# The second product of the attention scores over all 128 rows, in a two-layer decoder trunk

## The chip, the core and the metric

The kernel runs on one core of a Trainium2 chip, in one launch. The metric is the device time of that launch in microseconds (us), as the median of several runs; lower is better. The engines are TensorE (PE; its weight loads stand in a row of their own, PEld), VectorE (DVE), ScalarE (ACT), GpSimd (POOL) and SyncE (SP, which issues the loads from memory).

## What is computed

A trunk of two layers over 512 tokens of 1024 features, all float32: layer 0 is a gated linear recurrence and a gated FFN, layer 1 a differential attention and another gated FFN. The change lies in the scores of that attention. Each of its 8 heads has two components with keys and queries of 64 features each:

```python
def diff_attention(h, k, v, w_q, w_o, ..., rel_table, lambda_init):
    q = (h @ w_q).reshape(B, T, DA_HEADS, 2, DA_HEAD_DIM) * (DA_HEAD_DIM ** -0.5)   # 8 heads, 2, 64
    def block(args):                                                                # 128 tokens
        qb, bi = args
        bias = jnp.where((rel >= 0)[..., None], table[t5_bucket(rel)], -jnp.inf)
        s = jnp.einsum('bqhcd,bkhcd->bhcqk', qb, k) + bias
        p = jax.nn.softmax(s, axis=-1)
        attn = p[:, :, 0] - lam * p[:, :, 1]
        return jnp.einsum('bhqk,bkhv->bqhv', attn, v)
    ...
    o = rmsnorm(o, subln_g) * (1.0 - lambda_init)
    return o.reshape(B, T, DA_VDIM_TOTAL) @ w_o
```

## The kernel before

Everything is kept with the features on the 128 partitions and the 512 tokens along the row. To multiply float32 numbers exactly enough, a number is split into a high and a low part, both float32r, and a product is three matmuls: high by high, low by high, high by low (`mm3`, lines 102 to 104).

`attention` has a manual schedule: the instructions of PE, DVE, ACT and POOL run in the order in which the code issues them. First come the keys and queries of head 0. Then a loop goes over 32 blocks (8 heads of 4 blocks of 128 queries; block i of a head looks at its first n = 128 (i + 1) keys). In one turn, `scores(b + 2)` issues the scores of a block, `weigh(b + 1)` forms the attention weights on DVE (line 982), `turn(b)` transposes them on PE (line 989; ACT copies them back, line 991) and `gather(b)` multiplies them with the values (line 1002). Between these steps `units` issues pieces of the large products: keys K, queries Q and values V of the next heads, later the output product. Each of these needs a weight tile that SP loads, POOL multiplies by a gain (line 84), ACT rounds to the high part (line 756) and DVE subtracts for the low part (line 759). When a K or Q product is complete, DVE scales it out of PSUM (`evac`, line 825), and its parts are formed by steps that `some` issues one by one.

The queries of a head are a tile of two components, `qs`: component c has its high part on its own 64 rows and its low part on the other 64. The high part of the keys, `kh`, has for each component the same 64 features on both halves of the rows (ACT line 846, POOL line 847). So the first matmul of a component, line 958, contracts 128 rows and gives high by high and low by high at once. The low part of the keys, `kl`, is one tile of 128 rows by 512: rows 0 to 63 are component 0, rows 64 to 127 component 1 (DVE line 853). The second matmul, line 959, contracts 64 rows: the high part of the queries with the low part of the keys, added to the same PSUM bank. A block thus issues four matmuls in a row: 958, 959 for component 0, then 958, 959 for component 1. `kl` comes from a pool of two buffers.

Of the kernel before, what the change touches and what calls it, by code (L numbers as in the profile page):

```python
# [11 lines left out]
F32 = mybir.dt.float32  # L12
F32R = mybir.dt.float32r
# [21 lines left out]
class Trunk:  # L35
# [17 lines left out]
    def split(self, x, hi, lo, gain=None):  # L53
        """hi + lo = x (times gain), exact to float32, both in float32r."""
# [9 lines left out]
    def x_split(self, n, g, pool=None):  # L64
        """x^T tile n times a norm's gain, as two float32r parts"""
        pool = pool or self.xp
        g = None if g is None else self.gain(g, n)
        hi = pool.tile([P, T], F32R, tag="xs", name=f"xh{n}", bufs=2 * KD)
        lo = pool.tile([P, T], F32R, tag="xs", name=f"xl{n}", bufs=2 * KD)
        self.split(self.x[n], hi, lo, g)  # L70
        return hi, lo

    def stage(self, src, width=1024, gain=None, k0=0, cols=P):
        """weights from memory, times a gain of their input features"""
# [24 lines left out]
    def mm3(self, out, s, m, start, stop):  # L99
        """three passes of split operands; s stationary (hi, lo), m moving (hi, lo)."""  # L100
# [5 lines left out]
    def banks(self, ctx, name, **tags):  # L106
        """PSUM for a phase: tag -> (tiles, banks in a tile)"""
# [15 lines left out]
    def proj_first(self, items, xs, last, between=()):  # L123
        """several products at once, all but the last input tile first; between them, what else PE has to do"""
# [7 lines left out]
    def norm_steps(self, acc, name, tag):  # L132
        """the two parts of a norm as steps for proj_first; its result lands in the list"""
# [5 lines left out]
    def sq_add(self, acc, x, first, now=True):  # L139
        """acc += x^2; the sum is returned where it is not to be issued now"""  # L140
# [9 lines left out]
    def rsqrt_steps(self, out, ms, n):  # L150
        """out = ms ** -0.5 over the whole range: a guess from the exponent, three Newton steps"""
# [25 lines left out]
    def sums(self, acc, tag, chunks=range(4)):  # L177
        """sums over the features, by token"""
# [5 lines left out]
    def by_column(self, out, col):  # L184
        """out[p, t] = col[t] on every partition"""
# [40 lines left out]
    def begin(self, xs, acc, f_ps, q_ps):  # L226
        """the stream, its parts and its squares; head 0's first two products as the pieces come in"""
# [45 lines left out]
    def hgrn(self, xs, acc, on_tile):  # L273
        tc, nc, a, sp = self.tc, self.nc, self.a, self.sp
        v, s = nc.vector, nc.scalar
        with ExitStack() as ctx:
# [5 lines left out]
            # lower bound: softmax of two logits, first row; 1 - lb is the second  # L282
# [40 lines left out]
            def prep(h, f_ps, q_ps):  # L323
                """decay factors, keys and queries of every level."""
# [14 lines left out]
                # blocks of 4: types q0 q1 q2 q3 c1 c2 a2 c3 b3 a3, each over the 128 blocks  # L339
# [9 lines left out]
                # products over the blocks and what follows a place in its block  # L349
# [11 lines left out]
                # blocks of 16: types c0 c1 c2 c3 a2 a3 b3, each [32 blocks, 4 places]  # L361
# [5 lines left out]
                t4 = n16(tot)  # [p, child, block of 16]  # L367
# [19 lines left out]
                # blocks of 32, 64, 128  # L387
# [17 lines left out]
            def intra(h, vt, r1, r2, qs, ks, tt):  # L405
# [22 lines left out]
                # states at the chunks' ends  # L428
# [15 lines left out]
                # scores^T [key place, token], by chunk  # L444
# [4 lines left out]
                # level 1: ten types of 8 blocks  # L449
# [74 lines left out]
    def residual(self, w_src, ys, kt, on_tile, rb=None, late=False, extra=(), between=(), final=None):  # L524
        """x^T += (w^T y^T) (times rb by token); late: the last input tile comes last"""
# [30 lines left out]
    def last_tile(self, w_src, ys, kt, acc, out):  # L556
        """the last tile of the stream and the final norm, by halves of the tokens"""
# [32 lines left out]
        def factor(half):  # L590
            """1/rms of 256 tokens, as rsqrt but by column"""
# [17 lines left out]
        def spread(r):  # L609
            """for DVE and, in another bank, for the copy that GpSimd reads"""  # L610
# [89 lines left out]
    def bias_vector(self):  # L700
        """kept once for each of 128 tokens, so that a place less per token is a plain stride"""
# [544 lines left out]
```

## Time and profile before

| | |
|---|---|
| median of 3 runs | 1295.34 us (1295.14 to 1296.74) |
| span of the profiled execution | 1292.2 us |
| PE busy | 1263.4 us, 98% |
| PEld busy | 1043.4 us, 81% |
| DVE busy | 869.5 us, 67% |
| ACT busy | 568.1 us, 44% |
| POOL busy | 109.2 us, 8% |

The profile is of one execution. Its span runs from the first to the last instruction that the profiler saw; no other time is given for that execution, so what lies around the span is known only as the difference from the median, 1295.34 - 1292.2 = 3.1 us. A matmul's end is modelled, so PE's busy share says little on how tightly matmuls follow each other: for that the starts of successive rows are read. The attention's loop lies between about 664 and 898 us of the span.

### The profile page before, as it was taken

To read this page: it belongs to the slowest core of one execution; us is meant where nothing else is said; L and a number is where in the kernel's file an instruction comes from. 1 tells how busy PE (TensorE), PEld (TensorE's weight loads), DVE (VectorE), ACT (ScalarE), POOL (GpSimd) and SP (SyncE) were. 2 spreads that over 40 slices of the span, in tenths; PEclk is the share of its full clock that TensorE was granted. 3 is DMA by queue.
4 is the path that set the end of the run, shared out by engine and by line. 5 is a ranking of instruction groups with operands and counts; after the bars stand their busy time and mean duration, and the time that the engine had idled before them with its cause. 6 is when DMAs were issued, how large, how long until landed. Compare 5 with 4: busy or idle time off the path is not lost.

```text
span 1292.2 us, 18027 instructions
## 1 busy us (share of the span) xinstructions
PE 1263.4 (98%) x6994; PEld 1043.4 (81%) x6994; DVE 869.5 (67%) x1627; ACT 568.1 (44%) x986; POOL 109.2 (8%) x89
## 2 busy tenths in 40 slices
PE   8999899999999999999999999999999999999997
PEld 7888798778888888888887778787788888888886
DVE  7978689586777777523367878866687777772223
ACT  5554455454444444322245545554454444442221
POOL 3000000020000000000233332200200000000001
PEclk9999899999999999999999999999999999999999
DMA  6225322133333333333332212212233333333321
GB/s 207 82 84 82 100 69 80 50 114 99 98 98 98 96 96 95 93 90 90 94 98 61 78 50 57 74 59 65 76 120 99 98 98 98 98 90 90 91 88 66
DMA packets 37949, 115.35 MB, mean 89 GB/s; under 512 B 4032, under 2 KB 9448, under 8 KB 37864
## 3 DMA queue, kind: packets, MB, share of 16 engines
q1 hardware_dynamic: 36968, 113.29, 29.8%
q8 instruction: 55, 0.90, 0.3%
q10 hardware_dynamic: 896, 0.92, 0.2%
q14 instruction: 30, 0.25, 0.1%
HBM read 110.52 MB, written 3.67 MB: 88 GB/s over the span
## 4 chain that ended last, share of the span: by engine, by line
PE 57%; issue 30%; DVE 8%; DMA 3%; ACT 2%; SPq 0%; POOL 0%; POOLq 0%; DVEq 0%; ACTq 0%
PE mm L102 16%; PE mm L103 16%; PE mm L104 16%; DMA wst<-in_w_fqg_dram 2%; PE sc L959 1%; PE po L1002 1%; DVE wlo L58 1%; PE sc L958 1%; DVE wlo L759 1%; DVE sd L457 1%; DVE kl L853 1%; PE tp L989 1%; ACT whi L57 0%; DMA x<-in_x_t_dram 0%; PE sc L103 0%
## 5 line engine op out<-in xcount | busy, mean ns | idle before, releaser
L102 PE MATMUL mm<-xh,whi 128*128 128x512 f32 x1008 | 399.7, 397 | 0.5 <-ACT whi L57 0.5
L103 PE MATMUL mm<-xl,whi 128*128 128x512 f32 x1008 | 394.7, 392 | 2.5 <-DVE xl L61 2.3
L104 PE MATMUL mm<-xh,wlo 128*128 128x512 f32 x1008 | 394.3, 391 | 2.3 <-DVE wlo L58 2.3
L58 DVE TENSOR_TENSOR wlo<-wst,whi 128x1024 fp32r<-128x1024 f32 (+2 forms) x182 | 216.0, 1191 | 165.8 <-ACT whi L57 163.4
L57 ACT CAST whi<-wst 128x1024 fp32r<-128x1024 f32 (+2 forms) x182 | 181.8, 1003 | 257.5 <-PE mm L103 192.4
L104 PEld LDWEIGHTS mm<-xh,wlo 128*128 128x128 f32 x1008 | 189.8, 188 | 43.0 <-DVE wlo L58 3.4
L103 PEld LDWEIGHTS mm<-xl,whi 128*128 128x128 f32 x1008 | 190.1, 189 | 41.9 <-DVE xl L61 4.7
L102 PEld LDWEIGHTS mm<-xh,whi 128*128 128x128 f32 x1008 | 189.8, 188 | 41.0 <-issue 1.5
L102 PE MATMUL mm<-hh,whi 128*128 128x512 f32 (+1 forms) x374 | 142.8, 382 | 0.0
L103 PE MATMUL mm<-hl,whi 128*128 128x512 f32 (+1 forms) x374 | 142.6, 381 | 0.0
L104 PE MATMUL mm<-hh,wlo 128*128 128x512 f32 (+1 forms) x374 | 142.6, 381 | 0.0
L667 DVE TENSOR_TENSOR u<-mm,rbc_f 128x512 f32<-128x512 f32 x88 | 60.2, 688 | 73.5 <-PE mm L104 73.5
L147 POOL TENSOR_TENSOR acc<-acc,sq 128x512 f32<-128x512 f32 x18 | 26.7, 1482 | 669.2 <-ACT sq L146 669.1
L102 PEld LDWEIGHTS mm<-hh,whi 128*128 128x128 f32 x374 | 70.1, 188 | 15.2
L104 PEld LDWEIGHTS mm<-hh,wlo 128*128 128x128 f32 x374 | 70.1, 188 | 15.2
L103 PEld LDWEIGHTS mm<-hl,whi 128*128 128x128 f32 x374 | 70.1, 188 | 15.1
L669 ACT ACTIVATE c<-u,pack 128x512 f32<-128x512 f32 x88 | 71.5, 816 | 7.7 <-DVE u L667 4.0
L102 PE MATMUL mm<-whi,xh 128*128 128x256 f32 x256 | 74.7, 293 | 0.0
L103 PE MATMUL mm<-wlo,xh 128*128 128x256 f32 x256 | 72.4, 283 | 0.2 <-DVE wlo L759 0.2
L57 ACT CAST hh<-c 128x512 fp32r<-128x512 f32 x44 | 27.2, 619 | 102.9 <-DVE c L678 102.9
L104 PE MATMUL mm<-whi,xl 128*128 128x256 f32 x256 | 72.3, 283 | 0.0
L671 DVE SCALAR_TENSOR_TENSOR c<-u,pack,c 128x512 f32<-128x512 f32 x88 | 66.1, 751 | 2.8
(258 smaller groups left out, 1718.8 us busy)
## 6 DMA issues: line engine op xcount, KB each, us to landing
wst<-in_w_up_dram SPq DMA_DIRECT2D x88, 512.0 KB, 3.6
wst<-in_w_down_dram SPq DMA_DIRECT2D x32, 512.0 KB, 3.6
wst<-in_w_fqg_dram SPq DMA_DIRECT2D x22, 512.0 KB, 4.4
wst<-in_w_kq_dram SPq DMA_DIRECT2D x16, 512.0 KB, 3.7
wst<-in_w_down_dram SPq DMA_DIRECT2D x16, 384.0 KB, 3.2
wst<-in_w_i_dram SPq DMA_DIRECT2D x8, 512.0 KB, 4.4
wst<-in_w_ao_dram SPq DMA_DIRECT2D x8, 512.0 KB, 4.0
wst<-in_w_v_dram SPq DMA_DIRECT2D x8, 512.0 KB, 3.6
```

Source lines behind the costliest of these rows:

```text
L57: i = nc.scalar.copy(hi, x)
L58: j = nc.vector.tensor_tensor(lo, x, hi.bitcast(F32), ALU.subtract)
L102: mm(out, s[0], m[0], start=start, stop=False)
L103: mm(out, s[0], m[1], start=False, stop=False)
L104: mm(out, s[1], m[0], start=False, stop=stop)
L147: add = lambda engine=nc.vector: engine.tensor_tensor(acc, acc, sq, ALU.add)
L457: v.copy_predicated(dst, m, src)
L667: v.tensor_tensor(u[:, 2:], ps, rb, ALU.mult)
L669: s.activation(c, u[:, 2:], AF.Identity, bias=self.cb[:, layer, n:n + 1], scale=w(2))
L671: v.scalar_tensor_tensor(c, u[:, 0:T], w(0), c, ALU.mult, ALU.add)
L759: v.tensor_tensor(me.w[1], me.st, me.w[0].bitcast(F32), ALU.subtract)
L853: v.tensor_tensor(lo[own], k[own], hi[own, c].bitcast(F32), ALU.subtract))
```

## The change

The low part of the keys becomes a tile of two components, each 128 rows by 512: component c has the low part on its own 64 rows and zeros on the other 64. There are two such tiles, one for even and one for odd heads, allocated once; their zeros are written once by POOL before the loop, and DVE writes only the rows of each component's own half. The second matmul now contracts all 128 rows: the queries' high part meets the keys' low part, and the queries' low part meets zeros. The diff also strips comments and docstrings, which is left out here; with the added lines, 958 and 959 become 961 and 962, and 847 becomes 851.

```diff
             lower, upper = slice(0, 64), slice(64, 128)
             parts = ((lower, upper), (upper, lower))
+            kls = [ap.tile([P, 2, T], F32R, tag=f"kl{i}", name=f"kl{i}", bufs=1) for i in range(2)]
+            for t in kls:
+                for c, (own, other) in enumerate(parts):
+                    nc.gpsimd.memset(t[other, c].bitcast(F32), 0.0)
...
             def keys(h, ps):
                 k = evac(ps)
                 hi = ap.tile([P, 2, T], F32R, tag="kh", name="kh")
-                lo = ap.tile([P, T], F32R, tag="kl", name="kl")
+                lo = kls[h % 2]
...
                 for c, (own, other) in enumerate(parts):
                     side.append(lambda c=c, own=own:
-                                v.tensor_tensor(lo[own], k[own], hi[own, c].bitcast(F32), ALU.subtract))
+                                v.tensor_tensor(lo[own, c], k[own], hi[own, c].bitcast(F32), ALU.subtract))
...
                 for c in range(2):
-                    row = slice(64 * c, 64 * c + 64)
                     mm(sc[c], qs[h][:, c, oi], ks[h][0][:, c, 0:n], start=True, stop=False)
-                    mm(sc[c], qs[h][row, c, oi], ks[h][1][row, 0:n], start=False, stop=True)
+                    mm(sc[c], qs[h][:, c, oi], ks[h][1][:, c, 0:n], start=False, stop=True)
```

On PE, this is the order around the scores of a head's second block, rows of the kernel before with - and of the change with + (`sc` are the scores in PSUM, the shape is that of the result; how many rows are contracted does not show here):

```order
 L103 MATMUL mm<-wlo,xh_5497 128x256
 L104 MATMUL mm<-whi,xl_5498 128x256
-L958 MATMUL sc<-kh,qs 128x256
-L959 MATMUL sc<-kl,qs 128x256
-L958 MATMUL sc<-kh,qs 128x256
-L959 MATMUL sc<-kl,qs 128x256
+L961 MATMUL sc<-kh,qs 128x256
+L962 MATMUL sc<-kl_5943,qs 128x256
+L961 MATMUL sc<-kh,qs 128x256
+L962 MATMUL sc<-kl_5943,qs 128x256
```

Nothing moved on PE: the same matmuls stand at the same places, and the low part of the keys is now the fixed tile. On DVE, ACT and SP the order is the same too.

On POOL, this is the order at the start of the attention, ahead of and behind the clearing of the bias tile `nb` (`wst` is a weight tile times its gains, `kh` the copy of the keys' high part to the other half of the rows):

```order
 L84 TENSOR_TENSOR wst<-wst,gains 128x1024 x2
 L741 MEMSET nb 128x2x256
+L824 MEMSET kl_5943 64x512 x2
+L824 MEMSET kl_5944 64x512 x2
 L84 TENSOR_TENSOR wst<-wst,gains 128x1024
-L847 CAST kh<-kq 64x512 x2
+L851 CAST kh<-kq 64x512 x2
```

The four memsets that write the zeros stand between the clearing of `nb` and the next multiplication of a weight tile; all else on POOL keeps its place.

## Rows read from the trace of the kernel before

**Rows 1.** The page, part 1: busy time of each engine in us, share of the span, instructions.

```profile
PE 1263.4 (98%) x6994; PEld 1043.4 (81%) x6994; DVE 869.5 (67%) x1627; ACT 568.1 (44%) x986; POOL 109.2 (8%) x89
```

**Rows 2.** Busy time by window, four equal pieces of the attention's loop (two heads each): window, its length, then busy us (and instructions) of PE, PEld, DVE, ACT, POOL, the granted clock of TensorE, the DMA share and GB/s.

```profile
662.30:717.04 54.74, 53.99 (x283) 42.57 (x281) 42.41 (x83) 26.54 (x64) 23.23 (x15) 1.00 0.22 68
717.04:771.74 54.70, 52.58 (x292) 42.04 (x292) 44.79 (x111) 29.40 (x78) 17.40 (x11) 1.00 0.23 64
771.74:826.50 54.76, 52.69 (x295) 42.45 (x296) 44.71 (x116) 29.85 (x79) 15.32 (x10) 1.00 0.22 63
826.50:881.00 54.50, 53.96 (x301) 43.40 (x300) 39.66 (x121) 30.75 (x83) 1.22 (x2) 1.00 0.18 59
```

**Rows 3.** The timeline of PE around the scores of a block of 256 keys: start us, length us, engine, line, operation, names, rows*columns of the stationary operand, shape of the moving one.

```profile
676.04 0.28 PE L958 MATMUL sc<-kh,qs 128*128 128x256 f32 x1
676.25 0.38 PE L959 MATMUL sc<-kl,qs 64*128 64x256 f32 x1
676.56 0.38 PE L958 MATMUL sc<-kh,qs 128*128 128x256 f32 x1
676.87 0.38 PE L959 MATMUL sc<-kl,qs 64*128 64x256 f32 x1
677.19 0.39 PE L102 MATMUL mm<-whi,xh 128*128 128x256 f32 x1
677.41 0.28 PE L103 MATMUL mm<-wlo,xh 128*128 128x256 f32 x1
677.53 0.28 PE L104 MATMUL mm<-whi,xl 128*128 128x256 f32 x1
```

**Rows 4.** The same for a block of 512 keys, between products whose matmuls have 512 columns.

```profile
713.77 0.40 PE L958 MATMUL sc<-kh,qs 128*128 128x512 f32 x1
714.10 0.49 PE L959 MATMUL sc<-kl,qs 64*128 64x512 f32 x1
714.52 0.50 PE L958 MATMUL sc<-kh,qs 128*128 128x512 f32 x1
714.95 0.50 PE L959 MATMUL sc<-kl,qs 64*128 64x512 f32 x1
715.38 0.50 PE L102 MATMUL mm<-xh,whi 128*128 128x512 f32 x1
715.72 0.40 PE L103 MATMUL mm<-xl,whi 128*128 128x512 f32 x1
715.95 0.39 PE L104 MATMUL mm<-xh,wlo 128*128 128x512 f32 x1
```

**Rows 5.** The timeline of PE's weight loads in the same block of 512 keys; the bracket is the loader's idle time before.

```profile
714.10 0.18 PEld L959 LDWEIGHTS sc<-kl,qs 64*128 64x128 f32 x1 [0.37 <-issue]
714.52 0.19 PEld L958 LDWEIGHTS sc<-kh,qs 128*128 128x128 f32 x1 [0.24 <-issue]
```

**Rows 6.** The instructions of line 959 on PE: count, duration in ns (least, median, greatest), first and last start in us, and their forms.

```profile
L959 PE MATMUL sc<-kl,qs x64: 323/408/502, 670.4 to 877.3; 64*128 64x128 f32 x16, 64*128 64x256 f32 x16, 64*128 64x384 f32 x16, 64*128 64x512 f32 x16
```

**Rows 7.** The timeline of PE from 664 to 900 us, the rows in which it waited for another engine: the bracket is the idle time before the row and who ended it.

```profile
671.74 0.39 PE L103 MATMUL mm<-wlo,xh 128*128 128x256 f32 x1 [0.24 <-DVE wlo L759]
685.00 0.33 PE L989 MATMUL tp<-pack,at 128*128 128x128 f32 x1 [0.50 <-DVE at L982]
717.54 0.44 PE L989 MATMUL tp<-pack,at 128*128 128x128 f32 x2 [0.50 <-DVE at L982]
721.59 0.71 PE L1002 MATMUL po<-vt,aT 128*128 128x128 f32 x4 [1.55 <-ACT aT L991]
772.24 0.44 PE L989 MATMUL tp<-pack,at 128*128 128x128 f32 x2 [0.57 <-DVE at L982]
776.30 0.71 PE L1002 MATMUL po<-vt,aT 128*128 128x128 f32 x4 [1.57 <-ACT aT L991]
829.20 0.71 PE L1002 MATMUL po<-vt,aT 128*128 128x128 f32 x4 [0.54 <-ACT aT L991]
```

**Rows 8.** DVE's busy time by window, from where DVE takes a product out of PSUM to where PE's wait of rows 7 ends: window, length, busy us (and instructions), granted clock, DMA share, GB/s.

```profile
664.32:685.00 20.68, 18.55 (x25) 1.00 0.26 78
703.99:721.59 17.60, 17.00 (x36) 1.00 0.21 65
758.55:776.30 17.75, 17.15 (x36) 1.00 0.22 66
813.27:829.20 15.93, 15.33 (x36) 1.00 0.23 72
```

**Rows 9.** The timeline of DVE: the only idle time of DVE within the first of these windows, and the row that opens the second window.

```profile
675.75 2.73 DVE L759 TENSOR_TENSOR wlo<-wst,whi 128x1024 fp32r<-128x1024 f32 x1 [1.81 <-ACT whi L756]
703.99 0.69 DVE L825 SCALAR_TENSOR_TENSOR kq<-mm,rbc_n 128x512 f32<-128x512 f32 x1 [1.17 <-PE mm L104]
```

**Rows 10.** The timeline at the start of the attention, where the new memsets will stand: POOL and DVE.

```profile
651.61 0.52 POOL L741 MEMSET nb<- 128x512 f32 x1
653.69 2.17 POOL L84 TENSOR_TENSOR wst<-wst,gains 128x1024 f32<-128x1024 f32 x1 [1.56 <-DMA wst<-in_w_v_dram]
654.03 1.85 DVE L725 TENSOR_TENSOR lmp<-lm 64x2 f32<-64x2 f32 x1
684.19 0.61 POOL L847 CAST kh<-kq 64x512 fp32r<-64x512 f32 x1
```

## The prediction, made before the changed kernel ran

> **What bounds the kernel now.** I read the busy times first: PE is busy for 1263.4 us of the span, VectorE for 869.5 [rows 1]. The attention's loop, cut into four pieces of two heads, shows the same: PE 52.6 to 54.0 us of some 54.7, VectorE 39.7 to 44.8, at full granted clock [rows 2]. Only seven rows of PE in the whole loop waited for another engine, 5.5 us together [rows 7]. So the loop goes at PE's pace nearly everywhere, and the next engine, VectorE, stands close behind it in the middle two pieces (82%).
>
> A busy PE is not one that follows closely, so I then read the starts of successive matmuls around the scores. In an ordinary product a matmul of 256 columns starts 0.12 us after the one before (677.41 to 677.53), one of 512 columns 0.23 (715.72 to 715.95). Around the scores of 256 keys the starts lie 0.21, 0.31, 0.31, 0.32 and 0.22 apart, from the first matmul of line 958 to the second of the product that follows: 1.37 us for five matmuls that at the ordinary distance need 5 x 0.12 = 0.60 [rows 3]. With 512 keys it is 715.72 - 713.77 = 1.95 against 5 x 0.23 = 1.15 [rows 4]. So 0.77 and 0.80 us are lost, the same whatever the width: not a cost of columns, but one of order. It sits at the four places where a matmul with 64 rows follows one with 128, or the reverse. The loads show how: the loader idles 0.37 and 0.24 us and starts a load only when the matmul that uses it starts (714.10 in both rows), instead of during the matmul before [rows 4, 5]. Lines 102 to 104 also add several matmuls into one bank and lose nothing, and the first matmul of line 958 starts on time behind line 104's, so neither the bank nor the queries' tile is the cause.
>
> The Trainium skill has this as a rule (TensorEngine Tiling (Array Packing), section Tiling Modes): a change of tiling mode, rows being part of the mode, drains the engine. The trace agrees, at about 0.19 us for each of the four changes.
>
> **The change part by part.** *The second product over 128 rows.* All 64 matmuls of line 959 had 64 rows, two in each of 32 blocks [rows 6]; now no matmul of the loop changes the row count. The number of matmuls and their columns stay. I take the mean of the two blocks, 0.78 us, for all 32 (the 16 blocks of 128 and 384 keys lie on either side of the 256 and are taken to lose the same): 32 x 0.78 = 25.0 us of PE's time. That the new matmuls go at the ordinary distance is an assumption; lines 102 to 104 have that form and go at it.
>
> *What of it reaches the end.* Where PE waits for VectorE, a faster PE waits longer. I traced each wait [rows 7] back along VectorE. From the first product taken out of PSUM (664.32) to PE's wait that ends at 685.00, VectorE is busy 18.55 of 20.68 us, and its one idle time there, 1.81, is for ScalarE [rows 8, 9]: nothing in it waits for PE, so this stretch keeps its length. Scores of three blocks lie in it (blocks 0 to 2, at 670, 676 and 681 us), and what they save becomes waiting. The second stretch opens when PE ends a product (VectorE had idled 1.17 us for it at 703.99) and runs with VectorE 17.00 of 17.60 us busy until PE's wait ends at 721.59; the third and the fourth are like it (17.15 of 17.75, 15.33 of 15.93) [rows 8, 9]. Each opens at PE's pace, so what was saved before it is kept; but the scores of two blocks lie inside each, and theirs is lost. Lost: 3 + 3 x 2 = 9 blocks, 9 x 0.78 = 7.0 us. Kept: 23 blocks, 18.0 us. The waits [rows 7] should grow by about this sum, to some 12 us. Behind each stretch VectorE is later against PE than now; but there is no wait of PE between one stretch and the next [rows 7], so I let nothing more be lost there, and the last piece (VectorE 39.7 of 54.5 [rows 2]) keeps everything.
>
> *Four memsets on GpSimd.* Before this the queue clears `nb` in 0.52 us (128 rows of 512) and then idles 1.56 us for a weight tile that lands at 653.69 [rows 10]. Four memsets of 64 rows of 512 cost, by that row, 4 x 0.26 = 1.0 us if half the rows take half the time, 2.1 if the row's length alone counts, and 2.4 by the cast of the same shape (0.61). I take 2.1. So the multiplication by the gains starts 0 to 0.9 us later, 0.5 by my value. Its tile is used only far behind, but a tiny VectorE operation at 654.03 took 1.85 us, that is until this multiplication ended [rows 10], and the norm's sum follows it. Shifted with it, the norm would come up to 0.9 us later. If the tiny operation now goes first, while a memset runs, the norm comes earlier, by at most its 1.85 us. PE has other products there in either case. I take 0, with bounds of -1.8 and +0.9. Of this the Trainium skill says (SBUF — State Buffer, section Who interferes with whom) that a GpSimd instruction that only writes does not hold up a VectorE one with two inputs; no row here shows a memset beside one.
>
> *The keys' low part* is written by the same 16 subtractions of the same shape, into another place; the fixed tiles alternate by head as the two buffers did. Cost 0; what hides any shift is that a head's keys are complete a whole head before their first use.
>
> Sum: 1292.2 - 18.0 = 1274.2 us of span; with the 3.1 us by which the median lies above the span, 1277.3 us.
>
> **The rivals.** *All of it lands (A).* The stretches [rows 8] are not rigid: the same 36 instructions of VectorE are busy 17.15 us in one and 15.33 in another. Where GpSimd and VectorE meet otherwise than now, a stretch shrinks by up to 1.8 us, and two of them by that much give back 3.6 of the 7.0: 1273.7 us. With the whole saving it is 1295.3 - 25.0 = 1270.3 us. Against it: the shortest of the three still made PE wait.
>
> *VectorE takes over (B).* In the two middle pieces VectorE idles 54.7 - 44.8 = 9.9 us. If its queue needs that idle time (in fixed order it waits for ScalarE, which waits for PE and VectorE in turn), these 16 blocks save nothing, where I count 12 of them: 12 x 0.78 = 9.4 us less, 1286.7 us. For it: with 6.2 us off the piece, VectorE would be busy over 90% of it. Against it: most of VectorE's and ScalarE's waits there end with a PE row, so they shrink with PE.
>
> *No change (C).* The lost time is not from the row count but from something that stays, such as two loads of the same queries in a row. Then only the memsets count: 1295 to 1296 us. Against it stands the late load at each switch, and only there.
>
> *Slower (D).* A matmul of 64 rows leaves half of the array free, so that its neighbour can run beside it; widened, it takes its full turn. Then the change adds the ordinary distance of 64 matmuls: 128 and 384 keys by proportion 0.06 and 0.18, so 16 x (0.06 + 0.12 + 0.18 + 0.23) = 9.4 us, 1304.7 us. It decides only if some matmul starts sooner behind line 959 than the ordinary distance; all start later, by 0.19 at 256 keys [rows 3, 4]. The Trainium skill states the gain behind this rival (TensorEngine Tiling (Array Packing), section Theoretical Speedup): up to twice the speed for 64 rows, by two tiles side by side. This trace does not show it, since a 128-row matmul stands between any two.
>
> **How the numbers follow.** Forecast (1274 to 1281 us) 0.58; A (1270 to 1274) 0.14; B (1281 to 1289) 0.18; C 0.06; D 0.04. The predicted time is the forecast's, 1277.3. The range for 8 in 10 takes in A and the near half of B: 1270 to 1285. A measurement can tell about 0.2%, 2.6 us: faster 0.90, same 0.06, slower 0.04.
>
> **What would show it.** Right: the five starts from line 961 on lie 0.12 us apart at 256 keys and 0.23 at 512; the loader runs ahead through the scores; the two-head pieces [rows 2] take about 52, 50, 50 and 48 us (3, 6, 6 and 8 blocks kept); PE's waits for VectorE or ScalarE in the loop sum to about 12 us, at the same places. The layers before and after keep their lengths. The prediction is wrong if the starts at the switch stay at 0.31 (C), if PE waits at new places, for weight tiles above all (B), or if the norm at 652 to 664 us grows by more than 1 us.

## The result, and the profile after

The changed kernel took 1283.45 us (median of 4 runs, 1281.71 to 1285.22) against 1295.24 us of the kernel before on the same chip: 0.9906 of it, with an interval of 0.9889 to 0.9923. That is faster by 0.9%: 11.8 of the forecast 18.0 us, inside the range, and 6.2 us above the predicted 1277.3. The profiled execution has a span of 1282.0 us, 10.2 less than before.

Page of the kernel after, part 1; it answers to [rows 1]:

```profile
PE 1246.9 (97%) x6994; PEld 1045.2 (82%) x6994; DVE 869.2 (68%) x1627; ACT 567.9 (44%) x986; POOL 111.1 (9%) x93
```

PE has lost 16.5 us of busy time with the same number of matmuls; POOL has four instructions more, the memsets. PEld's busy time grew by 1.8 us; DVE and ACT changed by no more than 0.3.

PE's timeline around the scores, kernel after: a block of 128 keys, one of 256 (answers to [rows 3]), one of 512 (answers to [rows 4]). Columns as in those groups:

```profile
748.25 0.22 PE L961 MATMUL sc<-kh,qs 128*128 128x128 f32 x1
748.30 0.28 PE L962 MATMUL sc<-kl,qs 128*128 128x128 f32 x1
748.42 0.27 PE L961 MATMUL sc<-kh,qs 128*128 128x128 f32 x1
748.53 0.28 PE L962 MATMUL sc<-kl,qs 128*128 128x128 f32 x1
748.64 0.44 PE L102 MATMUL mm<-xh,whi 128*128 128x512 f32 x1
748.92 0.40 PE L103 MATMUL mm<-xl,whi 128*128 128x512 f32 x1
...
677.08 0.28 PE L961 MATMUL sc<-kh,qs 128*128 128x256 f32 x1
677.19 0.28 PE L962 MATMUL sc<-kl,qs 128*128 128x256 f32 x1
677.31 0.28 PE L961 MATMUL sc<-kh,qs 128*128 128x256 f32 x1
677.43 0.28 PE L962 MATMUL sc<-kl,qs 128*128 128x256 f32 x1
677.55 0.28 PE L102 MATMUL mm<-whi,xh 128*128 128x256 f32 x1
677.67 0.28 PE L103 MATMUL mm<-wlo,xh 128*128 128x256 f32 x1
...
711.81 0.39 PE L961 MATMUL sc<-kh,qs 128*128 128x512 f32 x1
712.04 0.39 PE L962 MATMUL sc<-kl,qs 128*128 128x512 f32 x1
712.26 0.39 PE L961 MATMUL sc<-kh,qs 128*128 128x512 f32 x1
712.49 0.39 PE L962 MATMUL sc<-kl,qs 128*128 128x512 f32 x1
712.72 0.39 PE L102 MATMUL mm<-xh,whi 128*128 128x512 f32 x1
```

At 256 and 512 keys the starts now lie 0.11 to 0.12 and 0.22 to 0.23 apart, the ordinary distance: the cost of the switches is gone. With 128 keys the matmuls have half the columns of those with 256, but only the second of the four follows in half the time (0.05 behind the first); the others lie 0.11 to 0.12 apart, so less could be saved there. The loader runs ahead through the scores, as forecast: the load for the matmul at 712.04 starts at 711.81.

PE's timeline, kernel after, the rows of the attention's loop in which PE waited for another engine; it answers to [rows 7]:

```profile
672.78 0.39 PE L103 MATMUL mm<-wlo,xh 128*128 128x256 f32 x1 [0.59 <-DVE wlo L759]
685.93 0.33 PE L992 MATMUL tp<-pack,at 128*128 128x128 f32 x1 [1.93 <-DVE at L985]
717.01 0.44 PE L992 MATMUL tp<-pack,at 128*128 128x128 f32 x2 [2.74 <-DVE at L985]
721.06 1.22 PE L1005 MATMUL po<-vt,aT 128*128 128x128 f32 x4 [0.59 <-ACT aT L994]
770.19 0.69 PE L992 MATMUL tp<-pack,at 128*128 128x128 f32 x2 [2.69 <-DVE at L985]
774.24 0.71 PE L1005 MATMUL po<-vt,aT 128*128 128x128 f32 x4 [0.28 <-ACT aT L994]
795.91 0.44 PE L992 MATMUL tp<-pack,at 128*128 128x128 f32 x2 [0.47 <-DVE at L985]
820.55 0.44 PE L992 MATMUL tp<-pack,at 128*128 128x128 f32 x2 [1.35 <-DVE at L985]
824.60 0.71 PE L1005 MATMUL po<-vt,aT 128*128 128x128 f32 x4 [1.53 <-ACT aT L994]
```

The waits sum to 12.2 us (before: 5.5), at the places of before and at two more, 795.91 and 820.55, both for DVE and neither for a weight tile. The one at 820.55 lies in the fourth stretch, which made PE wait before too (829.20 [rows 7]); the one at 795.91 lies in none.

Windows of the kernel after, from where DVE takes a product out of PSUM to where PE's wait ends; the columns are window, length, busy us (instructions) of PE, PEld, DVE, ACT and POOL, granted clock, DMA share, GB/s. They are the second, third and fourth stretch, each from the row that answers to that of [rows 8]. Behind them two windows in which the clock was down:

```profile
702.76:721.06 18.30, 14.97 (x70) 11.65 (x68) 17.35 (x36) 8.96 (x23) 8.88 (x5) 0.92 0.21 80
755.99:774.24 18.25, 15.29 (x69) 12.14 (x67) 17.30 (x36) 8.95 (x23) 9.22 (x5) 0.91 0.24 75
807.68:824.60 16.92, 14.04 (x70) 11.16 (x68) 15.97 (x36) 8.96 (x23) 6.22 (x4) 1.00 0.26 87
...
719.00:724.00 5.00, 4.41 (x15) 3.40 (x14) 4.62 (x12) 4.50 (x12) 0.00 (x0) 0.50 0.19 53
770.00:772.00 2.00, 1.81 (x6) 1.52 (x7) 1.84 (x7) 0.73 (x2) 0.00 (x0) 0.50 0.00 0
```

In these stretches DVE is busy 94 to 95% (before 96 to 97). They are now 18.30, 18.25 and 16.92 us long, where they were 17.60, 17.75 and 15.93 [rows 8]: 0.7, 0.5 and 1.0 longer, while PE has less to do in them. In each, 0.35 of the growth is idle time of DVE (0.95 against 0.60), the rest busy time. The first stretch opens at DVE's row at 665.35 in this trace and is 685.93 - 665.35 = 20.6 us long (20.7 before). The last two rows show a thing of this execution: at its two longest waits TensorE's granted clock fell to half (1.2 GHz), from 718.3 to 725.1, behind the wait that ended at 717.01, and from 769.5 to 772.9, beginning within the wait that ended at 770.19.

What the second stretch holds in the kernel after: rows of DVE and POOL in order of time, the bracket being idle time before the row.

```profile
705.65 2.48 DVE L759 TENSOR_TENSOR wlo<-wst,whi 128x1024 fp32r<-128x1024 f32 x1 [0.35 <-ACT whi L756]
...
709.70 4.13 POOL L84 TENSOR_TENSOR wst<-wst,gains 128x1024 f32<-128x1024 f32 x2
710.20 1.75 DVE L1028 TENSOR_SCALAR ome<-oms 128x4 f32<-128x4 f32 x1
711.98 1.88 DVE L158 TENSOR_SCALAR rs<-ome 128x4 int32<-128x4 int32 x1
713.89 0.16 DVE L162 SCALAR_TENSOR_TENSOR rs<-rs,ome 128x4 f32<-128x4 f32 x1
```

Two operations on 4 columns last 1.75 and 1.88 us; of such a size one lasts 0.16 (713.89). They end when POOL's two multiplications by the gains end (the later at 709.70 + 4.13 = 713.83). In the kernel before such standstills lie in the same stretch, but on other operations; rows of DVE and POOL in the kernel before:

```profile
704.98 1.90 POOL L84 TENSOR_TENSOR wst<-wst,gains 128x1024 f32<-128x1024 f32 x1 [4.82 <-DMA wst<-in_w_v_dram]
705.04 1.98 DVE L982 SCALAR_TENSOR_TENSOR at<-p,r 128x128 f32<-128x128 f32 x1
...
714.32 1.90 POOL L84 TENSOR_TENSOR wst<-wst,gains 128x1024 f32<-128x1024 f32 x1 [0.35 <-DVE rs L164]
714.41 1.82 DVE L163 TENSOR_TENSOR rs<-rs 128x4 f32<-128x4 f32 x1
```

In after these two operations take 0.35 and 0.16 us. Taken one by one, 29 of the 36 operations of each stretch keep their length within 0.01 us. The seven that change stand, in one kernel or the other, beside an instruction of POOL (a multiplication or a copy of `kh`); some grow, others shrink, and together they come to 0.3, 0.1 and 0.6 us more in the three stretches. Three such multiplications lie in the second and the third stretch, two in the fourth, before as after. The new idle time of 0.35 us is DVE's wait for ScalarE at 705.65; the third and the fourth stretch have the same row with the same wait. So a first reading of the loss is: POOL's multiplications make these stretches long, and a faster PE shifts the engines' work against each other in them. The Trainium skill (SBUF — State Buffer, section Who interferes with whom) says that VectorE and GpSimd share a pair of ports, which some VectorE operations can take, a `tensor_scalar` among them, and that whoever comes second is then blocked for the whole instruction; the rows of lines 1028 and 158 in after agree.

Where the time went by blocks, from the first matmul of a block's scores to that of another, saving against before in us; x1_rows is told below (the same second product over 128 rows, no memsets, no fall of the clock in its loop):

| from block to block | forecast | after | x1_rows |
|---|---|---|---|
| 0 to 3 (first stretch) | 0 | 0.1 | 0.9 |
| 3 to 6 | 2.3 | 2.1 | 2.2 |
| 6 to 8 (second stretch's end) | 0 | -2.2 | -0.7 |
| 8 to 14 | 4.7 | 3.5 | 4.1 |
| 14 to 16 (third) | 0 | -0.5 | -0.5 |
| 16 to 22 | 4.7 | 3.6 | 3.5 |
| 22 to 24 (fourth) | 0 | -1.0 | -1.0 |
| 24 to the span's end | 6.2 | 5.6 | 5.6 |
| sum | 18 | 11.2 | 14.0 |

The span of after gained only 10.2, since its first scores came 1.0 us later (671.23 against 670.20): 0.6 of that was there before the attention began, 0.5 arose between POOL's clearing of `nb` and the first scores.

### The profile page after: what moved, and what is told of

It is laid out like the page before. It is cut to its first block, busy times and chain, and to the rows that moved or that the text cites. A ratio compares the mean times of both kernels' runs of the same rounds, so it can differ in the third digit from the quotient of the medians.

```text
span 1282.0 us, 18032 instructions
## 1 busy us (share of the span) xinstructions
PE 1246.9 (97%) x6994; PEld 1045.2 (82%) x6994; DVE 869.2 (68%) x1627; ACT 567.9 (44%) x986; POOL 111.1 (9%) x93
## 4 chain that ended last, share of the span: by engine, by line
PE 53%; issue 30%; DVE 11%; ACT 3%; DMA 2%; POOL 0%; SPq 0%; POOLq 0%; ACTq 0%; DVEq 0%
PE mm L103 15%; PE mm L102 15%; PE mm L104 15%; DMA wst<-in_w_fqg_dram 2%; DVE wlo L759 1%; DVE kl L857 1%; PE po L1005 1%; DVE wlo L58 1%; ACT whi L756 1%; DVE sd L457 1%; DVE sc L964 1%; PE tp L992 1%; DVE qs L840 1%; ACT p L970 0%; ACT whi L57 0%
```

## The experiments

The theory after the result: the switches are gone as forecast, and what is missing was eaten by DVE's stretches, which POOL's multiplications fill with standstill. The rivals: the zeros and memsets cost it; the scores still lose something; the norm's small operations or ScalarE set the stretches' length; the clock.

**x1_rows.** In the kernel before, the second product takes all rows of the keys' old low part:

```diff
-                    mm(sc[c], qs[h][row, c, oi], ks[h][1][row, 0:n], start=False, stop=True)
+                    mm(sc[c], qs[h][:, c, oi], ks[h][1][:, 0:n], start=False, stop=True)
```

> The kernel before with one edit: the second matmul of a component contracts all 128 rows of the old tile of low parts. No zeros, no memsets, no new tiles; the low parts of the other component are added in, so this part of the scores is changed. Theory (the time lost was that of the switch between 64 and 128 rows, 0.77 us a block): the five starts at 256 keys lie 0.12 us apart as in the changed kernel, and the time is that of the changed kernel less the memsets' half microsecond, 1281 to 1285 us. Rival (the new tiles or their place bring the gain, or a part of it): the starts stay at 0.31, or the time lies above 1288 us.

1283.67 us against 1297.23, 0.9892 (0.9874 to 0.9910). The row count alone gives the whole gain of the change: the time shows no part of the zeros or of where the low part lies. PE's long waits are at the places of after: 2.74 and 1.53 us at 716.19 and 720.24, 2.68 and 1.53 at 767.29 and 771.34. The second of each pair is shorter in after (0.59 and 0.28), where PE ran at the half clock just before it. Here the clock did not fall, in the same stretch behind the same wait; window of x1_rows:

```profile
718.00:726.00 8.00, 6.47 (x37) 5.20 (x36) 7.87 (x22) 6.36 (x16) 0.00 (x0) 1.00 0.33 100
```

**x2_memsets.** The kernel before with the two new tiles and their memsets, which nothing reads:

```diff
+            kls = [ap.tile([P, 2, T], F32R, tag=f"kl{i}", name=f"kz{i}", bufs=1) for i in range(2)]
+            for t in kls:
+                for c, (own, other) in enumerate(parts):
+                    nc.gpsimd.memset(t[other, c].bitcast(F32), 0.0)
```

> The kernel before with the two new tiles and their four memsets added, which nothing reads. Theory: GpSimd's multiplication by the gains behind them ends about 1 us later, the tiny VectorE operation behind it too, and the time from the last FFN matmul to the first scores grows by 0.4 to 0.6 us; the rest of the loop is as before, 1295 to 1297 us. Rival (the 1.03 us by which the changed kernel's first scores start later is all the memsets'): that time grows by 1.0 us.

1294.95 us in one run, too little to tell 0.5 us by the time; the trace tells it. From the memset of `nb` to the first scores it is 672.03 - 652.99 = 19.04 us, and 18.59 before, 18.61 in x1_rows, 19.05 in after: the memsets cost 0.45. How, the kernel after shows at the start of the attention (POOL and DVE; answers to [rows 10]):

```profile
652.18 0.52 POOL L741 MEMSET nb<- 128x512 f32 x1
652.76 2.23 POOL L824 MEMSET kl<- 64x512 f32 x4
653.47 1.23 DVE L759 TENSOR_TENSOR wlo<-wst,whi 128x1024 fp32r<-128x1024 f32 x1 [0.21 <-ACT whi L756]
654.61 2.25 DVE L725 TENSOR_TENSOR lmp<-lm 64x2 f32<-64x2 f32 x1
654.97 1.89 POOL L84 TENSOR_TENSOR wst<-wst,gains 128x1024 f32<-128x1024 f32 x1
```

The four memsets take 2.23 us, the multiplication starts 0.7 later against `nb` and ends 0.4 later, and DVE's tiny operation again stands until its end, the norm's sum behind it. The memsets themselves hold nobody up: DVE's subtraction beside them keeps its 1.23 us. The Trainium skill states that too (SBUF — State Buffer, the same section: GpSimd instructions that only write).

**x6_memsets_late.** The kernel after with the memsets written behind the norm's steps in the code:

```diff
-            for t in kls:
-                for c, (own, other) in enumerate(parts):
-                    nc.gpsimd.memset(t[other, c].bitcast(F32), 0.0)
...
                 live.clear()
+                for t in kls:
+                    for c, (own, other) in enumerate(parts):
+                        nc.gpsimd.memset(t[other, c].bitcast(F32), 0.0)
```

> The changed kernel with the four memsets issued behind the norm's products instead of ahead of them; nothing else differs. Theory (they cost the 0.46 us by which the first scores come later against the clearing of the bias tile): from that clearing to the first scores 18.6 us instead of 19.05, and about 0.5 us less time, which is inside the noise: 1281 to 1285 us. Rival (the memsets cost more, through later places of GpSimd's queue): over 1.5 us less.

1283.61 us against 1295.93, 0.9911 (0.9896 to 0.9926): as after. The edit moved nothing, because POOL has nothing between the two places; the memsets stand right behind `nb` again, at 654.70, and `nb` to first scores is 19.03 us.

So this run did not test what it was meant for. It serves as a second profile of the change: with the clock full in the loop, it saved 622.0 - 608.4 = 13.6 us from the first scores on, and its blocks 6 to 8 took 16.1 us, where after took 17.6. By this comparison (1.5 us there, 0.6 more in blocks 8 to 14) the fall of the clock cost after's profiled execution about 2 us.

**x3_order.** The kernel before with the two matmuls of 64 rows next to each other (958, 958, 959, 959), that is with two switches in a block instead of four:

```diff
                 for c in range(2):
-                    row = slice(64 * c, 64 * c + 64)
                     mm(sc[c], qs[h][:, c, oi], ks[h][0][:, 0:n], start=True, stop=False)
+                for c in range(2):
+                    row = slice(64 * c, 64 * c + 64)
                     mm(sc[c], qs[h][row, c, oi], ks[h][1][row, 0:n], start=False, stop=True)
```

> The kernel before with one edit: the two matmuls of line 958 first, then the two of line 959, all else as it was. Two changes of the row count a block instead of four. Theory (each change costs 0.19 us, and two matmuls of 64 rows one behind the other cost the ordinary distance): at 256 keys the starts from the first matmul on lie 0.12, 0.21, 0.12, 0.31 and 0.22 apart, 0.39 us a block are saved, 12 us of PE's time, of which VectorE's stretches take a third or more: 1286 to 1290 us. Rival (two matmuls on the two halves of the rows run side by side): the second of line 959 starts less than 0.05 us behind the first, 0.15 us a block more are saved, 1283 to 1287 us. Rival (the loss belongs to the change of the PSUM bank or of the queries' tile): the sum of the starts stays at 1.37 us and the time at 1295.

1287.85 us against 1297.23, 0.9927 (0.9912 to 0.9942): faster than before, slower than after. PE's timeline around a block of 256 keys; a row with x2 holds two matmuls that the view put together:

```profile
677.62 0.40 PE L957 MATMUL sc<-kh,qs 128*128 128x256 f32 x2
677.94 0.38 PE L960 MATMUL sc<-kl,qs 64*128 64x256 f32 x2
678.26 0.39 PE L102 MATMUL mm<-whi,xh 128*128 128x256 f32 x1
678.48 0.28 PE L103 MATMUL mm<-wlo,xh 128*128 128x256 f32 x1
```

Two switches, two late starts: the five starts take 678.48 - 677.62 = 0.86 us (the first matmul of line 957 starts at 677.62), where it was 1.37 with four switches and is 0.59 with none. The two matmuls of 64 rows, each on its own half of the rows, start at the same moment. That is the first rival's mark: its sum of the starts was 0.83, the theory's 0.98; the time lies in the theory's range. So the mechanism of rival D exists; in the kernel before, a 128-row matmul between them kept it from working. With the Trainium skill's gain for 64 rows, up to twice the speed (TensorEngine Tiling (Array Packing), section Theoretical Speedup), this pair agrees: it starts as one. The order of x3_order saves one distance (0.12 us at 256 keys) and costs two switches of about 0.2 each: 0.59 - 0.12 + 2 x 0.2 = 0.87. The rows of zeros, without any switch, save more.

**x4_nogain_after and x5_nogain_before.** The kernels after and before without POOL's multiplications of line 84:

```diff
-            self.nc.gpsimd.tensor_tensor(w, w, g, ALU.mult)
+            pass
```

> The changed kernel without GpSimd's multiplications of the attention's weights by their gains, which are left out of the result. Theory (VectorE's stretches have grown because its operations with two inputs in SBUF stand still while GpSimd multiplies a weight tile, 1.6 us each in two tiny operations of the second stretch): the stretches that take 18.3, 18.3 and 16.9 us come down to 12 to 15, PE's waits in the loop fall from 12 to under 4 us, TensorE's clock stays at its upper level there, and the time is 1274 to 1279 us. Rival (VectorE's own work sets them): the stretches stay over 16 us, PE waits over 8 us, the time stays over 1280 us.

> The kernel before without GpSimd's multiplications of the attention's weights by their gains, which are left out of the result: the control for the changed kernel without them, which took 1266.6 us. Theory (the two effects need each other: before, the switches of PE hide most of VectorE's standstills): only PE's 5.5 us of waits go, 1288 to 1292 us, so that the change is worth 22 to 25 us where GpSimd does not multiply, against 12 where it does. Rival (GpSimd's multiplications cost some 17 us by themselves): 1277 to 1283 us.

After without them: 1266.6 us against 1297.23, 0.9765 (0.9748 to 0.9781). Before without them: 1288.47 against 1295.93, 0.9949 (0.9934 to 0.9964). In neither does PE wait for another engine anywhere in the loop; here a window of somewhat over two heads of the kernel x4_nogain_after, with PE busy throughout:

```profile
714.27:767.50 53.23, 53.23 (x334) 47.53 (x333) 43.19 (x129) 34.77 (x93) 5.73 (x8) 1.00 0.26 80
```

x4_nogain_after lies 7 us below even its theory's range (1274 to 1279), x5_nogain_before within its own. This settles the main question. Without POOL's multiplications the change is worth 1288.47 - 1266.6 = 21.9 us, with them 11.8. The two ran on different chips; each taken against the kernel before on its own chip, it is (1297.23 - 1266.6) - (1295.93 - 1288.47) = 23.2. A period of 8 blocks takes 46.3 us instead of 52.1: nothing is given back. And since PE alone sets the pace here, the saving of a block can be read by its width, from the first matmul of the scores to the second matmul of the product behind them: 1.25 to 0.67 us at 128 keys, 1.48 to 0.70 at 256, 1.72 to 0.94 at 384, 1.95 to 1.15 at 512. That is 0.58, 0.78, 0.78 and 0.80, on average 0.73.

**x8_chain_gpsimd.** The kernel after with the small steps of the norm that stand in the stretches (12 operations of 128 x 4 a head, which become 15) on POOL instead of DVE; the rewritten square root is left out here:

```diff
-                chain.append(lambda: v.tensor_scalar(me, ms, 1.0 / P, EPS, ALU.mult, ALU.add))
-                chain.extend(self.rsqrt_steps(r, me, 4))
-                chain.append(lambda: v.tensor_tensor(r, r, r0, ALU.mult))
+                chain.append(lambda: g.tensor_scalar(me, ms, 1.0 / P, EPS, ALU.mult, ALU.add))
+                chain.extend(self.pool_rsqrt_steps(r, me, 4))
+                chain.append(lambda: g.tensor_tensor(r, r, r0, ALU.mult))
```

> The changed kernel with the small steps of the heads' norm (128 by 4, some 12 a head) on GpSimd instead of VectorE. Theory (in the second stretch two of these steps stand still for 1.75 and 1.88 us behind GpSimd's multiplications, and the rest take 1.5 us): the stretches shorten by 3 to 5 us, PE's waits fall from 12 to 4 to 8 us, the time is 1276 to 1280 us. Rival (the standstill moves to the next operation of VectorE that meets GpSimd, which now also works longer): stretches and waits as they were, 1282 to 1287 us.

1283.89 us against 1295.93, 0.9910 (0.9894 to 0.9927): no change against after. The standstill goes to the next operation of DVE, and on POOL the first step starts only behind the multiplication, at 715.86:

```profile
713.88 1.89 POOL L84 TENSOR_TENSOR wst<-wst,gains 128x1024 f32<-128x1024 f32 x1
713.97 2.09 DVE L1008 SCALAR_TENSOR_TENSOR at<-p,r 128x256 f32<-128x256 f32 x1
```

PE then waits for the norm's result itself, six times by 0.36 to 1.70 us, where it did not before. So relief for these small operations gains nothing: another operation of DVE runs into POOL's. Not every one is held up, though: in the kernel before, the two operations of line 961, which read the scores from PSUM, keep their 0.56 and 0.60 us at 711.96 and 712.44, beside the multiplication that starts at 712.07.

**x10_scale_act.** The kernel after with the scaling of `o` (DVE, 0.68 us in each stretch) on ACT, in four pieces:

```diff
-                chain.append(lambda: v.tensor_tensor(by_token, by_token, r.unsqueeze(2).broadcast_to([P, 4, P]),
-                                                     ALU.mult))
+                for i in range(4):
+                    chain.append(lambda i=i: s.activation(by_token[:, i], by_token[:, i], AF.Identity, scale=r[:, i:i + 1]))
```

> The changed kernel with the scaling of a head's output by its norm (one VectorE operation of 128x512, 0.68 us a head) done by ScalarE in four operations of 128x128. Theory (VectorE's queue sets the stretches, ScalarE has room): each stretch shortens by about 0.7 us, the time falls by 1.5 to 2.5 us to 1281 or 1282. Rival (ScalarE's queue is on the same chain, through the exponentials and the transposed weights): no change or slower, 1283 to 1286 us.

1290.64 us (9 runs) against 1295.93, 0.9958 (0.9947 to 0.9969): 7 us slower than after, and slower than even the rival's 1283 to 1286. PE's wait for ACT's copy in the fourth stretch:

```profile
832.83 0.71 PE L1005 MATMUL po<-vt,aT 128*128 128x128 f32 x4 [2.68 <-ACT aT L994]
```

Where after waited 1.53, 2.68 us are waited now, and in the third stretch 2.72 instead of 0.28 (1.53 in x1_rows and x6_memsets_late, without the fall of the clock): the four pieces (1.28 us together at 721.64) stand in ACT's queue ahead of the copy that PE needs. ScalarE is on the same chain, so relief for DVE at ACT's cost makes it longer. A part of the 7 us may be the clock's: in this profile it stood at half for 17 us of the loop (after: 10), and the one run with a mean clock of 0.993 took 1286.79 us.

**x7_fill.** The kernel after with 23 matmuls of 512 columns more, before PE's turn of blocks 5, 13 and 21, that is in the waits:

```diff
+                for _ in range({5: 9, 13: 9, 21: 5}.get(b, 0)):
+                    mm(tp, qs[b // 4][:, 0, 0:P], ks[b // 4][0][:, 0], start=True, stop=True)
```

> The changed kernel with idle-time matmuls: 9, 9 and 5 extra matmuls of 128x512, about 2.1, 2.1 and 1.2 us, ahead of the three transposes at which PE waits longest (2.74, 2.69, 1.35 us), into the bank that the transposes then fill. Theory (part of the loss is TensorE's clock, which in the changed kernel's profile stands at half for some 7 and 3 us behind these waits): the clock stays at its upper level through the loop and the time falls by 1 to 3 us, to 1280 to 1282 us. Rival (VectorE sets the end anyway, so a slow PE behind the wait costs nothing): the clock stays up but the time is 1283 to 1285 us.

1282.29 us against 1296.62, 0.9882 (0.9861 to 0.9903). By the ordinary distance 23 x 0.23 = 5.3 us of work were added to PE, at no cost: its interval and after's overlap. The time lies between the ranges of theory and rival and decides for neither. PE's wait in the second stretch is shorter by what fills it, 0.63 us instead of 2.74, and ends at the same transposes:

```profile
718.24 0.44 PE L994 MATMUL tp<-pack,at 128*128 128x128 f32 x2 [0.63 <-DVE at L985]
```

So in the stretches PE's time is worth nothing. Whether the filling keeps the clock up can't be told: it was full in this profile's loop, but also in those of x1_rows and x6_memsets_late without it.

**x11_fold.** The kernel after with fewer multiplications on POOL: the gain of keys and values is put on the stream once, where it is split, and the queries' weights are multiplied by the ratio of the two gains. Only 8 of the 24 multiplications stay. It needs a gain of keys and values without zeros.

```diff
-            K = [[Load(a["w_kq"][2 * h], 2)] for h in range(NH)]
-            Q = [[Load(a["w_kq"][2 * h + 1], 3)] for h in range(NH)]
-            V = [[Load(a["w_v"][p, hf], 2, 4 * hf, 256) for hf in range(2)] for p in range(NH // 2)]
+            K = [[Load(a["w_kq"][2 * h])] for h in range(NH)]
+            Q = [[Load(a["w_kq"][2 * h + 1], 7)] for h in range(NH)]
+            V = [[Load(a["w_v"][p, hf]) for hf in range(2)] for p in range(NH // 2)]
...
+        nc.vector.reciprocal(inv, t.gains[:, 2])
+        nc.vector.tensor_tensor(t.gains[:, 7], t.gains[:, 3], inv, ALU.mult)
...
-        xs, acc, nxt = nxt[0], nxt[1], stage("plain")
+        xs, acc, nxt = nxt[0], nxt[1], stage(2)
```

> The changed kernel with the gains of keys and values put on the stream's split (ScalarE and VectorE form it anyway, with a scale it costs 0.07 us a tile each) instead of on their weights; the queries' weights are multiplied on GpSimd by the ratio of the two gains. 8 of GpSimd's 24 multiplications in the attention stay. Theory (VectorE's standstills behind GpSimd's multiplications are what the change loses in the stretches): PE's waits in the loop fall from 12 us to under 5, the stretches to 13 to 16 us, the time to 1267 to 1274 us. Rival (the 8 that stay fall into the same stretches and stop the same operations): waits over 8 us, 1277 to 1283 us.

1267.8 us against 1296.62, 0.9774 (0.9753 to 0.9796): better than both kernels, and within 1.2 us of x4_nogain_after, which has no multiplication at all. The only wait of PE above 0.2 us that is left in the loop is the one at its start (0.59 at 672.38, as in after at 672.78).

From block 8 to block 24 it takes 807.91 - 715.39 = 92.5 us, where after took 102.1 and before 107.6.

**x12_four_buffers.** The kernel after with four buffers instead of three for the weight tiles as loaded, so that their loads can run ahead further. It asks why the stretches grew:

```diff
-        st = self.wp.tile([P, 1024], F32, tag="wst", name="wst", bufs=3)
+        st = self.wp.tile([P, 1024], F32, tag="wst", name="wst", bufs=4)
```

> The kernel after with four buffers instead of three for the weight tiles as they come from memory, so that a tile can be loaded before the low part of the third one back is formed. In the kernel after, the first multiplication by the gains in each of the three stretches of VectorE waits for its tile and starts 2.0, 1.6 and 3.5 us behind the stretch's opening row (before: 1.0, 1.1 and 1.1), and VectorE idles 0.35 us more. Theory (the stretches grew because the weight tiles, whose loads did not come earlier by as much as PE, arrive later in them): the first multiplication comes earlier against the opening, at most 1.2 us behind it, the idle time of 0.35 goes, the three stretches shrink to about 17.6, 17.7 and 15.9 us, and the time falls by about 2 us, to some 1281.5. Rival (only the number of multiplications in a stretch counts): they start earlier but stand in VectorE's way all the same; the stretches stay within 0.2 us of 18.3, 18.25 and 16.9 and the time at 1283 to 1284. Third: with an early tile the multiplication falls ahead of the opening and a stretch loses one whole multiplication of 1.9 us, some 4 us in all.

1280.84 us (1277.97 to 1282.68) against 1296.77, 0.9878 (0.9856 to 0.9900): the interval overlaps that of after, so the gain isn't certain. The theory's own mark did not come: the first multiplication starts 2.7, 2.2 and 3.5 us behind the opening, no earlier than in after. But the stretches became shorter. From the opening row to PE's wait at the transposes it is 13.86 and 13.79 us in the second and third, where after has 14.25 and 14.20 and before 13.55 and 13.69; the fourth, to its wait at the product, is 15.16 us (after 16.92, before 15.93). Rows of DVE and POOL in x12_four_buffers, the second and the fourth stretch:

```profile
703.13 4.04 DVE L759 TENSOR_TENSOR wlo<-wst,whi 128x1024 fp32r<-128x1024 f32 x2
...
807.07 2.76 POOL L84 TENSOR_TENSOR wst<-wst,gains 128x1024 f32<-128x1024 f32 x1 [1.41 <-ACT kh L850]
811.13 0.17 DVE L1028 TENSOR_SCALAR ome<-oms 128x4 f32<-128x4 f32 x1
```

In the second and the third stretch the two subtractions now follow each other without the 0.35 us of waiting for ScalarE, which is what they shrank by (0.4). In the fourth only one multiplication is left of two, the small operations run at 0.17 us, and it is 1.76 us shorter, about one multiplication: the expectation's third case, some 4 us in all, came in this one stretch. So in this profile a stretch's length goes by the multiplications that fall into it and by DVE's wait for ScalarE, and two of the three shrank although their first multiplication came no earlier. Against these gains a new wait of 1.63 us stands in the first stretch, so that from the first scores on this profile saves 622.0 - 607.8 = 14.2 us, hardly more than x1_rows. It is the fastest of the four runs, and the clock fell three times in its loop, for 3.4 us each.

## Why the prediction came out, and where it was off

- **The cost of the switch** was right in place and size: 1.37 us became 0.59 at 256 keys and 1.95 became 1.14 at 512, the forecast distances. That it is the change of row count is shown twice: x1_rows changes nothing else and has the same gain, and in x3_order two switches instead of four take 0.86 us, that is 0.39 above the 0.47 that four distances need, and 0.39 is half of the 0.78 lost with four. Rival C has fallen.
- **0.78 us for all blocks** was too much for the narrow ones: 0.58 with 128 keys (x4 and x5). Forecast as 32 x 0.78 = 25.0, the saving is 8 x (0.58 + 0.78 + 0.78 + 0.80) = 23.5 us; the two profiles without multiplications differ by 23.2 from the first scores on. Seven of the 23 blocks that count are narrow, so it is 7 x 0.2 = 1.4 us.
- **The stretches** were found rightly: what is saved inside them becomes waiting. PE's waits came to 12.2 us, about 12 forecast, and added work in them costs nothing (x7_fill). **"These stretches keep their length" is the step that failed**: three of the four grew, by 0.7, 0.5 and 1.0 us, which is lost in full, and one more wait, 0.47 us at 795.91, came up where none had been, against "nothing more is lost there". Together 2.7 of the missing us. Of the signs named for being wrong, a wait at a new place came, but for DVE and not for a weight tile. That the length depends on how POOL and DVE meet was said under rival A, but only in the direction of a gain. That POOL's multiplications make the stretches bound PE is shown (x4, x11). Of the growth, 0.35 us in each is DVE's new wait for ScalarE, which x12 took away with that effect in the second and the third. The rest lies, by the rows, in the seven operations of each that stand beside POOL's work; why they come to more and not to less in all three stretches stays open.
- **Memsets at 0** was wrong by 0.45 us; the multiplication, for which 0.5 was estimated, started 0.7 later and ended 0.4 later, and the norm followed it, as the upper bound allowed.
- **The clock.** I took it as full in the loop. It fell twice in the profiled execution, for about 2 us of loss; x1_rows and x6_memsets_late show the same waits without a fall, x3_order, x10_scale_act and x12_four_buffers show one to three falls in the loop. What decides it, and how often it falls in the runs without a trace, isn't known; of the changed kernel's four runs, the two with a mean clock of 0.989 took 1283.88 and 1285.22 us, the one with 0.993 took 1281.71.
- **Sum.** Of the 18.0 us, 11.2 arrived behind the first scores in the profiled execution (10.2 of the span, with the first scores 1.0 later), 14.0 and 13.6 in the two profiles without the fall of the clock. Of the 4.0 that x1_rows misses, 2.7 are the stretches and the new wait and 1.4 the narrow blocks, 0.9 came back in the first stretch, and the other 0.8 lie in small amounts in the pieces of the table. After's profile has 2.8 less than x1_rows: 2.1 where the clock fell, and some 0.8 in the first stretch, for which no run shows the reason. That the time lies inside the range is owed to its upper end, which was set by the near half of rival B, a mechanism that did not come.
- **Rivals.** A would have needed shorter stretches. B (1286.7) is nearer by the number, 3.3 us above the result, but not by its mechanism: it let the 16 middle blocks save nothing, and between the stretches they kept 3.5 us in six (0.6 each). D's mechanism is real, but not in the order of the kernel before.

## What to carry to other kernels

Read the distance of successive starts, not busy time, to find matmuls that lose at a change of row count; adding rows of zeros to keep one count paid more here than putting matmuls of the same count together. Then look for where another engine sets the pace and ask what fills it: nearly half of the gain went into stretches of VectorE that were long because GpSimd worked beside it, and taking away two thirds of GpSimd's multiplications in the attention gave 16 us. Don't take such a stretch as rigid when the engine that feeds it becomes faster; here they grew by 3 to 6%.

## What was not expected of the hardware

- Two matmuls of 64 rows on different halves, issued one behind the other, start at the same moment (677.94 in x3_order, where the ordinary distance is 0.12).
- Of four matmuls of 128 columns in a row, the second starts 0.05 us behind the first, but the next two 0.11 to 0.12 apart, as those of 256 columns do (0.12).
- VectorE operations on 4 columns, in place of 0.16 us, last up to 1.88 us beside a GpSimd multiplication of 1.9 us.
- TensorE's granted clock fell to one half behind a wait of 2.74 us in after (718 to 725), and behind one of 2.30 in x3_order (719 to 722); it stayed full in x1_rows and x6_memsets_late behind waits of 2.74 and 2.69 us at the same place.
